# Dilated attention with every engine's queue in written order, and its small work handed out between dense products

## The chip, the cores and the metric

The kernel runs on one core of a Trainium2 chip. The metric is the device time of one execution in microseconds. A core has five engines with queues of their own, each worked off in order: TensorE (PE; its weight loads, PEld, overlap the matmuls), VectorE (DVE), ScalarE (ACT), GpSimd (POOL) and SyncE (SP). The last issues most DMAs here; ScalarE issues some too, and then does so from the same queue as its arithmetic. Engines wait for one another by semaphores. What stands behind a waiting instruction in a queue waits with it.

## The reference, cut to what matters

One encoder block with 1024 tokens of width 1024: a norm, one wide input projection, three mixers side by side (dilated window attention A, grouped-query attention B, cross-attention M), a gate for each, three merged projections, an output projection and a norm. The change is in mixer A:

```python
A_GROUPS = ((128, 1), (512, 4), (2048, 16))     # window, dilation
for gi, (window, dil) in enumerate(A_GROUPS):
    hs = slice(gi * A_HEADS, (gi + 1) * A_HEADS)
    o_g, lse_g = dilated_window_attention(aq[:, :, hs], ak[:, :, hs], av[:, :, hs], window, dil)
    ...
wts = jax.nn.softmax(jnp.stack(lses, axis=0), axis=0)
oa = jnp.einsum('gbsh,gbshd->bshd', wts, jnp.stack(outs, axis=0))
```

There are 8 heads of 64 channels in each group. Queries and keys are rotated by position (rope). In a group a query attends to the tokens at multiples of the dilation inside its window; the three groups' outputs are weighed by a softmax over their log-denominators.

## The kernel before

**Dense products in three passes.** Every float32 weight tile is split into a rounded high part and the rest (`split`, L104: a copy on ScalarE, a subtraction on VectorE), and so are the tokens. A unit (`add_unit`) is 128 output channels: two halves of 512 tokens, each 8 blocks of the width times three matmuls, so 24 matmuls (L143, L145, L147) into one of two PSUM banks `d`. Then the half is evacuated, and its bank is free again.

**The dilated stage** works through 12 items: four pairs of heads (`p_`), each in the three groups (`g` = 0, 1, 2). An item has eight tiles of 128 queries. For each tile there are: `scores` (four tiles at a time, TensorE, into four PSUM banks), `soft` (on VectorE the mask and the maximum; on ScalarE the exponential with its sum, for two heads), `trans` (TensorE turns the probabilities, ScalarE copies them out as `app`), and `pv` (values' products for four tiles, TensorE; ScalarE copies `og`). `stats` turns the row sums and maxima once for an item (L1359). The outputs of `trans`, `pv` and `stats` share two PSUM tiles. The transposes run two tiles behind the softmax, so the last two tiles, the second `pv` and the statistics of an item fall into the next one.

**What is woven.** `weave` (L174) sets TensorE's order by hand: it walks through the pieces of an item (`plan`, L1396), each with a cost, and through the matmuls of one dense unit, and takes the next matmul whenever the attention's share of its cost is ahead. The dense unit of item n makes the rotated queries of item n + 2 (`q_rope`: four products of 32 rows on VectorE, L1194, one of 128 rows, L1195, an addition on GpSimd, L1196); four gate units follow at the end. Keys come ready from HBM as two tiles (`kraw`, `kswp`), which GpSimd adds (`k_add`, L1223). Values come in blocks (`avs`, `avp`). After each third group, `combine` fetches the statistics, makes the weights (`weights`, L1471, a chain of short VectorE steps with one exponential on ScalarE), sends them through HBM (`wgd`, `wgt`) and weighs three outputs (`weigh`, L1491).

**What sets the order of the other engines.** The first two units run under a manual schedule, that is, in the order in which the code issues. All after it, to the end of the stage, is ordered on VectorE, ScalarE, GpSimd and SyncE by a scheduler that goes by priorities and estimated readiness; `issue_after` ties combining to the latest softmax step. The weights of a unit are loaded and split whole (1024 columns at once) when `prepare` reaches them, one unit ahead. Buffers `wr` for raw weights are two.

**The value stage**, earlier, from 456 us, makes the values with a scheme of seven block products. It starts with a write of reciprocals (`rld`, L829) from SyncE's queue, then eight weight loads `vA` (L857). `sum_at` (L894) issues its sums of weight blocks on GpSimd.

Of the kernel before, what the change touches and what calls it, by code (L numbers as in the profile page):

```python
# [16 lines left out]
NT = 8  # L17
# [33 lines left out]
def block(ctx: ExitStack, tc: tile.TileContext, x, xT, memT, cst, msk, bcst, tabA, gpost,  # L51
# [121 lines left out]

    def weave(count, att=None, att_cost=0.0, lead=1.0, prio=ATT_PRIO):  # L174
        dg = run_items(count)
        dc = cost_items(count)
        d = a = 0.0
        live_d, live_a = True, att is not None
        while live_d or live_a:
            if live_d and (not live_a or a / att_cost >= min(1.0, d / dc * lead)):  # L180
                try:
                    d += next(dg)
                except StopIteration:
                    live_d = False
                    d = 1e18
            else:
                try:
                    with tc.high_priority(offset=prio):
                        a += next(att)
                except StopIteration:  # L190
                    live_a = False
# [466 lines left out]
    with tc.tile_pool(name="ba", bufs=1, reuse_waits="tile") as ba:  # L658
# [170 lines left out]
        nc.sync.dma_start(rld.rearrange("h (a b) -> (h a) b", b=64), rl)  # L829
# [139 lines left out]

    BK = {}  # L970
# [58 lines left out]
    for n, (i, e, k) in enumerate(steps_v):  # L1029
# [76 lines left out]
    for n in range(6):  # L1106
        for i, (an, bn) in enumerate(PRODUCTS):
# [9 lines left out]
            if i == 0:  # L1117
                if n:
                    k_block(n, "S2")
                k_block(n, "A22")  # L1120
                if n < 5:
                    k_load(n + 1, 0)
            elif i == 1:
                k_block(n, "S4")
                if n < 5:
                    k_load(n + 1, 1)
            elif i == 2:
                k_block(n, "S1")
            elif n == 5:
                if i == 3:  # L1130
                    early[len(queue)] = lambda: [wp.tile([P, 1024], F32, name="wr", bufs=WR)]
                    prepare(len(queue))
                    nc.sync.dma_start(ready[len(queue)][0], wu[0])
                elif i == 6:
                    raw = ready.pop(len(queue))[0]
                    w = wslot(0), wslot(1)
                    split(*w, raw)
                    ready[len(queue)] = tuple(z.rearrange("p (k f) -> p k f", k=8) for z in w)
# [28 lines left out]
    with tc.tile_pool(name="aa", bufs=1, reuse_waits="tile") as aa:  # L1167
# [19 lines left out]
        def q_rope(o, half, p, g):  # L1187
# [4 lines left out]
            for a in range(4):  # L1192
                i, j = slice(32 * a, 32 * a + 32), slice(32 * (a ^ 1), 32 * (a ^ 1) + 32)
                V.scalar_tensor_tensor(t2[i], p[j], -0.125, tab[1][j, t], op0=OP.mult, op1=OP.mult)  # L1194
            fp["last"] = V.scalar_tensor_tensor(t1, p, -0.125, tab[0][:, t], op0=OP.mult, op1=OP.mult)  # L1195
            G.tensor_tensor(half_of(o, half, g), classes(t1, g), classes(t2, g), op=OP.add)  # L1196

        def add_a(p_, g):
# [7 lines left out]
            add_unit(wu[(p_ * 3 + g) * 2], evac)  # L1206
# [18 lines left out]
        def item(p_, g):  # L1225
# [130 lines left out]
            def stats():  # L1356
# [24 lines left out]
            size = [window(g, T)[1] - window(g, T)[0] for T in range(NT)]  # L1381
# [4 lines left out]
                scores=[(lambda b=b: scores(b), 350 + sum(size[4 * b:4 * b + 4]) * 4 / 2.4) for b in range(2)],  # L1386
                soft=[(lambda T=T: soft(T), 300.0) for T in range(NT)],
                trans=[(lambda T=T: trans(T), 109.0 * {128: 2, 192: 3, 256: 4}[size[T]]) for T in range(NT)],
                pv=[(lambda b=b: pv(b), 250.0 + sum(213.0 * len(blocks_of(T)) for T in range(4 * b, 4 * b + 4))) for b in range(2)],
                stats=(stats, 109.0))  # L1390

        def joined(*pieces):
            pieces = [x for x in pieces if x]
            return (lambda: [fn() for fn, _ in pieces]), sum(c for _, c in pieces)

        def plan(it, pre, nxt):  # L1396
# [3 lines left out]
            def combining(T):  # L1400
                while todo and T == STEP_T[-len(todo)]:
                    with tc.issue_after(fp["last"].ins):
                        todo.pop(0)()

            def tokens(T):
                if T >= 2:
                    for nm, k in late[:2]:
                        with tc.issue_after(fp["last"].ins):
                            split_block(nm, k)
# [109 lines left out]
        def first_blocks():  # L1519
            load_pair(0, 0)  # L1520
            load_pair(0, 1)
            own_blocks(0)

# [17 lines left out]
        seq = [(p_, g) for p_ in range(4) for g in range(3)]  # L1541
        add_a(*seq[0])
# [3 lines left out]
        k_fetch(*seq[0])  # L1546

        def first_keys():
            yield 300.0
# [4 lines left out]
            yield 300.0  # L1554

        weave(2, first_keys(), 1000.0)
        manual.__exit__(None, None, None)
        items = [item(*x) for x in seq] + [None]
        for n in range(len(seq)):
            if n + 2 < len(seq):  # L1560
                add_a(*seq[n + 2])
            elif n + 2 == len(seq):
                for j in GATES_A:
                    add_gate(*j)
                early[len(queue)] = first_blocks
# [13 lines left out]
            weave(len(GATES_A) - 1 if last else 1, run(pieces), sum(c for _, c in pieces), 1.0)  # L1579

# [335 lines left out]
G_AT = 4  # L1916
# [115 lines left out]
```

## Time and profile before

| what | value |
|---|---|
| median of 3 runs | 1476.32 us (1474.78 to 1477.55) |
| profiled execution, its own time | 1477.48 us |
| its span, first to last instruction | 1475.7 us |
| mean granted TensorE clock | 0.991 |
| TensorE busy | 1419.1 us, 96% of the span |
| VectorE, ScalarE, GpSimd busy | 998.7, 651.6, 523.1 us |
| dilated stage | about 706 to 1039 us |
| TensorE idle from 717 to 727 us | 9.8 us, one wait |
| TensorE idle from 741 to 1040 us | 19.5 us, 24 waits |

Times are counted from the first instruction. A busy share of TensorE includes matmuls at a lowered clock, so the granted clock (1.00 is full speed) belongs beside it. A group's row gives its line in the kernel, the engine, the operation, the output and inputs, the count, the busy time, the mean of one in ns, and the idle time just before it with what ended it. Line numbers are those of the kernel before; in the changed kernel the same code stands 6 lines lower in the value stage and some 15 to 55 lower in the dilated stage.

### The profile page before, as it was taken

The numbers are of one execution on the slowest core, as the hardware profiler recorded it, in microseconds if no ns is written. First come the engines' busy times: TensorE is split into PE (matmuls) and PEld (weight loads), VectorE is DVE, ScalarE is ACT, GpSimd is POOL, SyncE is SP. The second block draws the span as 40 slices with busy tenths as digits, with TensorE's granted clock in tenths as the row PEclk, the third lists the DMA queues.
The fourth block names the chain that finished last, engine by engine and source line by source line (L and its number), as shares of the span: only waits on it lengthen the run. The fifth ranks groups of instructions, "written<-read, shape, count | busy, mean of one in ns | idle before, by whom it ended". The sixth has DMA issues, their size and how long they took to land.

```text
span 1475.7 us, 21171 instructions
## 1 busy us (share of the span) xinstructions
PE 1419.1 (96%) x7556; PEld 1133.2 (77%) x7556; DVE 998.7 (68%) x1737; ACT 651.6 (44%) x1407; POOL 523.1 (35%) x402
## 2 busy tenths in 40 slices
PE   7999999999999899999799998999999999999998
PEld 7899986666666788888577767778887888888887
DVE  7755468777752974888565676675688788559643
ACT  6544365665653443321056564665433444213221
POOL 1425405676763402332143343430234331035322
PEclk9999999999999999999899999999999999999999
DMA  6332022223113688344533343453433543857122
GB/s 239 102 108 72 30 80 82 69 94 97 52 39 137 198 262 272 125 170 172 181 91 112 97 138 111 124 150 108 143 124 118 181 175 113 291 209 266 55 98 100
DMA packets 112985, 198.67 MB, mean 135 GB/s; under 512 B 23984, under 2 KB 53744, under 8 KB 112880
## 3 DMA queue, kind: packets, MB, share of 16 engines
q1 hardware_dynamic: 86816, 166.78, 34.5%
q10 hardware_dynamic: 26064, 30.55, 5.9%
q8 instruction: 59, 0.97, 0.3%
q14 instruction: 46, 0.38, 0.1%
HBM read 142.40 MB, written 54.89 MB: 134 GB/s over the span
## 4 chain that ended last, share of the span: by engine, by line
PE 68%; DVE 12%; ACT 7%; DMA 5%; issue 4%; POOL 3%; SPq 1%; ACTq 0%; DVEq 0%; POOLq 0%
PE s L125 16%; PE sc L125 9%; PE d L147 6%; PE d L145 6%; PE d L143 5%; PE sc L1878 5%; PE s L1040 4%; PE ov L755 3%; ACT pra L1303 3%; DVE t2a L1194 2%; PE s L739 2%; PE tr L721 2%; PE s L740 2%; PE d L536 2%; DMA wr<-in_wu 1%
## 5 line engine op out<-in xcount | busy, mean ns | idle before, releaser
L143 PE MATMUL d<-hh,wh 128*128 128x512 f32 x480 | 196.6, 410 | 11.5 <-DVE t1a L1195 9.8
L147 PE MATMUL d<-hh,wl 128*128 128x512 f32 x480 | 196.3, 409 | 0.0
L145 PE MATMUL d<-hl,wh 128*128 128x512 f32 x480 | 194.4, 405 | 0.0
L746 POOL TENSOR_TENSOR bl<-bl,bp 128x512 f32<-128x512 f32 x96 | 131.5, 1369 | 53.6 <-ACT bp L742 48.1
L105 ACT ACTIVATE wh<-wr 128x1024 fp32r<-128x1024 f32 (+1 forms) x75 | 67.3, 898 | 177.3 <-PE sc L125 76.0
L125 PE MATMUL sc<-hh,wh 128*128 128x512 f32 x384 | 118.4, 389 | 0.0
L143 PEld LDWEIGHTS d<-hh,wh 128*128 128x128 f32 x480 | 91.9, 191 | 33.0 <-issue 15.2
L145 PEld LDWEIGHTS d<-hl,wh 128*128 128x128 f32 x480 | 92.2, 192 | 21.6 <-issue 6.3
L147 PEld LDWEIGHTS d<-hh,wl 128*128 128x128 f32 x480 | 91.6, 191 | 22.1 <-issue 5.0
L1194 DVE SCALAR_TENSOR_TENSOR t2a<-d,tab 32x512 f32<-32x512 f32 x96 | 66.0, 687 | 56.6 <-PE d L147 54.9
L106 DVE TENSOR_TENSOR wl<-wr,wh 128x1024 fp32r<-128x1024 f32 x47 | 70.6, 1503 | 44.9 <-ACT wh L105 44.4
L1303 ACT ACTIVATE pra<-pra,sts 128x192 f32<-128x192 f32 (+2 forms) x192 | 84.2, 439 | 34.7 <-DVE sts L1302 34.6
L722 DVE TENSOR_REDUCE bn<-tr 128x1 f32<-128x512 f32 x128 | 86.1, 686 | 17.5 <-PE tr L721 16.1
L742 ACT ACTIVATE bp<-s 128x512 f32<-128x512 f32 x128 | 75.9, 595 | 46.8 <-PE s L740 45.7
L106 DVE TENSOR_TENSOR ch<-sf,ch 128x512 fp32r<-128x512 f32 x68 | 59.0, 869 | 44.4 <-ACT ch L105 44.3
L1196 POOL TENSOR_TENSOR aq<-t1a,t2a 128x512 f32<-128x512 f32 x24 | 43.8, 1825 | 123.7 <-DVE t1a L1195 103.7
L125 PEld LDWEIGHTS sc<-hh,wh 128*128 128x128 f32 x384 | 72.1, 188 | 15.1
L105 ACT ACTIVATE ch<-sf 128x512 fp32r<-128x512 f32 x68 | 41.6, 628 | 93.8 <-PE s L125 46.3
L1605 POOL TENSOR_TENSOR sf<-wr 128x512 f32<-128x512 f32 x22 | 30.6, 1409 | 144.2 <-DMA wr<-in_wu 61.4
L1809 POOL TENSOR_TENSOR acc<-acc,th 128x1024 f32<-128x1024 f32 x15 | 40.9, 2728 | 108.8 <-DVE th L1808 106.1
L125 PE MATMUL s<-hh,ch 128*128 128x512 f32 x224 | 74.1, 392 | 1.7 <-ACT ch L105 1.7
L125 PE MATMUL sc<-hl,wh 128*128 128x512 f32 x192 | 74.7, 389 | 0.0
(389 smaller groups left out, 3731.3 us busy)
## 6 DMA issues: line engine op xcount, KB each, us to landing
wr<-in_wu SPq DMA_DIRECT2D x64, 512.0 KB
kd<-kr ACTq DMA_DIRECT2D x48, 256.0 KB
th<-thd SPq DMA_DIRECT2D x24, 512.0 KB
thd<-rs ACTq DMA_DIRECT2D x44, 256.0 KB
g2d<-fth SPq DMA_DIRECT2D x24, 256.0 KB
kraw<-kd SPq DMA_DIRECT2D x12, 512.0 KB
kswp<-kd SPq DMA_DIRECT2D x48, 128.0 KB
wgt<-wgd SPq DMA_DIRECT2D x24, 256.0 KB
```

Of the source, the lines that this page charges most:

```text
L105: A.activation(dst_h, src, AF.Copy)
L106: V.tensor_tensor(dst_l, src, dst_h.bitcast(F32), op=OP.subtract)
L125: PE.matmul(out_ps, a, b, start=i == 0, stop=i == n - 1)
L143: PE.matmul(dst, wh[:, k, :], hh[k][:, t], start=k == 0, stop=False)
L145: PE.matmul(dst, wh[:, k, :], hl[k][:, t], start=False, stop=False)
L147: PE.matmul(dst, wl[:, k, :], hh[k][:, t], start=False, stop=k == 7)
L722: fp["last"] = V.tensor_reduce(st[i]["n"][:, j, c:c + 1], s, axis=AX.X, op=OP.min)
L742: A.activation(pp, s, AF.Exp, scale=-1.0)
L746: G.tensor_tensor(lsum[i % 2], lsum[i % 2], pp, op=OP.add)
L1194: V.scalar_tensor_tensor(t2[i], p[j], -0.125, tab[1][j, t], op0=OP.mult, op1=OP.mult)
L1303: A.activation(src, src, AF.Exp, scale=-1.0, bias=bias, accum_out=sts[:, h, 1, T:T + 1])
L1878: PE.matmul(parts[h], *terms[h][j], start=j == 0, stop=j == 23)
```

## The change

1. From the first two units to the end of the dilated stage, the manual schedule stays on for VectorE, ScalarE, GpSimd and SyncE: their queues hold the order in which the code issues. The `issue_after` ties and the empty piece before the statistics go.
2. A list `pend` takes small pieces: the five VectorE steps of each rotation, the two steps of each gate evacuation, and the next unit's weight split in two halves of 512 columns. `weave` issues the next of them after every third dense matmul.
3. The weights of the stage's 16 units have a list of their own (`AU`): each is fetched two units ahead, the first two already during the last key products; its split is handed out in the second half of the unit before.
4. The costs in `plan` no longer follow TensorE's time: a softmax step counts 1000, a joined piece (values' products and next scores) 300, a transpose 100. So the dense matmuls are spread over softmax steps.
5. In the value stage, the write `rld` goes out from ScalarE's queue, and the sums S3 and S4 are issued one step later.

```diff
+    pend = []
...
     def weave(count, att=None, att_cost=0.0, lead=1.0, prio=ATT_PRIO):
...
                     d += next(dg)
+                    steps += 1
+                    if pend and steps % 3 == 0:
+                        pend.pop(0)()
...
-        nc.sync.dma_start(rld.rearrange("h (a b) -> (h a) b", b=64), rl)
+        nc.scalar.dma_start(rld.rearrange("h (a b) -> (h a) b", b=64), rl)
...
+    def a_fetch(n):
+        AR[n] = wp.tile([P, 1024], F32, name="wr", bufs=WR)
+        nc.sync.dma_start(AR[n], wu[AU[n]])
+
+    def a_split(n, x):
+        if x == 0:
+            AW[n] = wslot(0), wslot(1)
+        split(*[z[:, half[x]] for z in AW[n]], AR[n][:, half[x]])
...
-        for nm, s0 in (("S1", 2), ("S3", 7), ("S4", 11)):
+        for nm, s0 in (("S1", 2), ("S3", 8), ("S4", 12)):
...
+            pend.extend([lambda a=a: cross(a) for a in range(4)] + [straight])
+
+        def add_au(evac):
+
+            n = next(counter)
+
+            def gen(_):
+                if n + 2 < len(AU):
+                    a_fetch(n + 2)
+                else:
+                    load_pair(0, n + 2 - len(AU))
+                for half in range(2):
+                    p = psd()
+                    if half and n + 1 < len(AU):
+                        pend.extend(lambda x=x: a_split(n + 1, x) for x in range(2))
+                    elif half:
+                        pend.append(lambda: own_blocks(0))
+                    w = [z.rearrange("p (k f) -> p k f", k=8) for z in AW[n]]
+                    yield from dense(w, half, p)
+                    evac(half, p)
+            queue.append((lambda: None, gen, UNIT))
...
-                soft=[(lambda T=T: soft(T), 300.0) for T in range(NT)],
-                trans=[(lambda T=T: trans(T), 109.0 * {128: 2, 192: 3, 256: 4}[size[T]]) for T in range(NT)],
+                soft=[(lambda T=T: soft(T), SOFT) for T in range(NT)],
+                trans=[(lambda T=T: trans(T), 100.0) for T in range(NT)],
...
-                    out += [(lambda: None, 300.0), pre["stats"]]
+                    out.append(pre["stats"])
...
         weave(2, first_keys(), 1000.0)
-        manual.__exit__(None, None, None)
...
+        while pend:
+            pend.pop(0)()
+        manual.__exit__(None, None, None)
...
+SOFT, JOINED = 1000.0, 300.0
```

**SyncE, where the dilated stage begins.** `in_wu` is the array of weights, `kd` holds the finished keys, `in_msk` the mask. Before:

```order
L1170 DMA mask<-in_msk 128x768
L1213 DMA kraw<-kd 128x1024
L1216 DMA kswp<-kd 32x1024 x4
L114 DMA wr<-in_wu 128x1024 x4
L1213 DMA kraw<-kd 128x1024
L1216 DMA kswp<-kd 32x1024 x4
```

Now, with the key stage's weight loads above the mask:

```order
L974 DMA wr<-in_wu 128x1024 x10
L982 DMA wr<-in_wu 128x1024 x3
L1185 DMA mask<-in_msk 128x768
L1266 DMA kraw<-kd 128x1024
L1269 DMA kswp<-kd 32x1024 x4
L1266 DMA kraw<-kd 128x1024
L1269 DMA kswp<-kd 32x1024 x4
L982 DMA wr<-in_wu 128x1024 x2
```

Three weight loads of this stage now stand ahead of the mask and of the first key tiles; before, all behind them.

**TensorE, around the statistics of an item** (`pra` are probabilities, `sts` the statistics). Before:

```order
L1329 MATMUL tr<-cs,pra 128x128 x4
L143 MATMUL d<-hh_87,wh 128x512
L145 MATMUL d<-hl_95,wh 128x512
L147 MATMUL d<-hh_87,wl 128x512
L1320 MATMUL tr<-cs,pra 128x128 x3
L143 MATMUL d<-hh_88,wh 128x512
L1359 MATMUL tr<-cs,sts 32x128
L145 MATMUL d<-hl_96,wh 128x512
```

Now:

```order
L1382 MATMUL tr<-cs,pra 128x128 x4
L143 MATMUL d<-hh_88,wh 128x512
L145 MATMUL d<-hl_96,wh 128x512
L147 MATMUL d<-hh_88,wl 128x512
L143 MATMUL d<-hh_89,wh 128x512
L145 MATMUL d<-hl_97,wh 128x512
L147 MATMUL d<-hh_89,wl 128x512
L1373 MATMUL tr<-cs,pra 128x128 x3
L1412 MATMUL tr<-cs,sts 32x128
```

Six dense matmuls stand between two tiles' transposes where there were three, and none before the statistics where there was one. The 12 to 14 that stood ahead of each values' product are now one or two.

**ScalarE at the same place** (two `pra` are one tile's exponentials, `app` the copy of turned probabilities, `sr` of the statistics). Before:

```order
L1354 ACTIVATE og<-tr 128x512
L1303 ACTIVATE pra,sts<-pra,sts 128x192 x6
L1332 ACTIVATE app<-tr 128x512
L1303 ACTIVATE pra,sts<-pra,sts 128x192
L1362 ACTIVATE sr<-tr 32x128
L1332 ACTIVATE app<-tr 128x384
```

Now:

```order
L1407 ACTIVATE og<-tr 128x512
L1356 ACTIVATE pra,sts<-pra,sts 128x192 x2
L1385 ACTIVATE app<-tr 128x512
L1356 ACTIVATE pra,sts<-pra,sts 128x192 x2
L1385 ACTIVATE app<-tr 128x384
L1415 ACTIVATE sr<-tr 32x128
```

The first copy stood behind three tiles' exponentials and now stands behind one tile's.

More of the change, by code (lines that the diff above doesn't have):

```diff
@@ L177, in weave @@
         d = a = 0.0
+        steps = 0
         live_d, live_a = True, att is not None
@@ L1129, in block @@
             elif n == 5:
[L1130 to L1138, printed above, removed]
+                for x_ in range(2 if i == 6 else 0):
+                    a_split(0, x_)
             elif i == 3:
@@ L1204, in evac, with add_ag, first, second @@
                 q_rope(d["q"], half, p, g)
-            add_unit(wu[(p_ * 3 + g) * 2], evac)
+            add_au(evac)
+        def add_ag(i, p_):
+            def evac(h, p):
+                th = aa.tile([P, 512], F32, name="fth", bufs=2)
+                def first():
+                    V.tensor_tensor(th, p, rb[:, half[h]], op=OP.mult)
+                    A.activation(p, th, AF.Tanh, scale=0.5)
+                def second():
+                    V.scalar_tensor_tensor(th, p, 1.0, th, op0=OP.add, op1=OP.mult)
+                    nc.sync.dma_start(g2d[i, p_, :, half[h]], th)
+                pend.extend([first, second])
+            add_au(evac)
         KK = {}
@@ L1401, in combining @@
                 while todo and T == STEP_T[-len(todo)]:
-                    with tc.issue_after(fp["last"].ins):
-                        todo.pop(0)()
+                    todo.pop(0)()
             def tokens(T):
@@ L1407, in tokens @@
                     for nm, k in late[:2]:
[L1408 to L1409 removed]
+                        split_block(nm, k)
                     del late[:2]
@@ L1563, in block @@
                 for j in GATES_A:
-                    add_gate(*j)
-                early[len(queue)] = first_blocks
+                    add_ag(*j)
             last = n + 1 == len(seq)
```

34 lines of the change are left out of this document (18 added, 16 removed).

## The prediction

> **What bounds the kernel now.** I read the page first, then the stretches of the dilated stage, then who TensorE waits for there.
>
> ```profile
> span 1475.7 us, 21171 instructions
> PE 1419.1 (96%) x7556; PEld 1133.2 (77%) x7556; DVE 998.7 (68%) x1737; ACT 651.6 (44%) x1407; POOL 523.1 (35%) x402
> ```
>
> TensorE sets the time: all that can be won without removing matmuls is the 56.6 us in which it is idle, and what a low clock costs after idling. The dilated stage runs from 706 to 1039 us. Per stretch (length, busy time of PE, PEld, DVE, ACT, POOL with instruction counts, then the granted clock, DMA share, GB/s):
>
> ```profile
> 717.00:727.00 10.00, 0.18 (x2) 0.03 (x1) 6.01 (x8) 2.11 (x2) 0.00 (x0) 0.71 0.52 176
> 727.00:742.00 15.00, 15.00 (x58) 11.98 (x58) 8.43 (x13) 1.07 (x1) 9.90 (x7) 0.86 0.25 76
> 742.00:780.00 38.00, 35.22 (x263) 28.15 (x264) 26.14 (x83) 20.81 (x71) 13.45 (x8) 0.96 0.33 98
> 780.00:857.00 77.00, 70.91 (x546) 55.85 (x546) 47.83 (x143) 44.48 (x146) 26.28 (x15) 0.98 0.41 114
> 857.00:928.00 71.00, 64.83 (x501) 51.00 (x497) 48.42 (x142) 40.24 (x133) 26.50 (x14) 0.98 0.43 121
> ```
>
> No helper is full: VectorE is busy 48 of 71 us where TensorE loses 6. So these are waits for order and latency. TensorE's waits between 741 and 1040 us (total, times, longest), and the one at the start:
>
> ```profile
> PE tr L1359 <- ACT app L1332: 12.3, 10, 2.8
> PE tr L1320 <- ACT app L1332: 3.1, 4, 1.3
> PE tr L1329 <- ACT app L1332: 2.5, 8, 0.5
> PE tr L1320 <- ACT pra L1303: 1.6, 2, 1.0
> PE d L143 <- DVE t1a L1195: 9.8, 1, 9.8
> ```
>
> **The start of the stage.** The 9.8 us have a cause in SyncE's queue:
>
> ```profile
> 709.41 0.33 SPq L1213 DMA_DIRECT2D kraw<-kd  x1
> 712.01 12.37 SPq L114 DMA_DIRECT2D wr<-in_wu  x4
> 719.74 1.06 ACT L105 ACTIVATE wh<-wr 128x1024 fp32r<-128x1024 f32 x1 [17.61 <-DMA wr<-in_wu]
> 720.83 1.23 DVE L106 TENSOR_TENSOR wl<-wr,wh 128x1024 fp32r<-128x1024 f32 x1 [10.30 <-ACT wh L105]
> ```
>
> The weights of the second unit stand behind the key tiles, which wait for the stage before; VectorE's split of them stands ahead of the first rotation, and that rotation holds the PSUM bank. After the wait the matmuls step by 0.43 us before they return to 0.23:
>
> ```profile
> 727.56 0.63 PE L145 MATMUL d<-hl,wh 128*128 128x512 f32 x1
> 727.99 0.63 PE L147 MATMUL d<-hh,wl 128*128 128x512 f32 x1
> ```
>
> From the clock 0.86 over 15.00 us that costs 15.00 x 0.14 = 2.1 us. The change fetches the first two units' weights during the key products, and puts the second split behind the first rotation: five steps of 0.69 us (rows below) and two half splits are 4.9 us beside the next 24 dense products of 0.23, 5.5 us. They fit. **Term 1: -9.8 - 2.1 = -11.9 us.** If the cover fails (the first scores then wait for the keys, which GpSimd adds only after those same transfers), up to all of it comes back.
>
> **The waits inside the stage.** Most are the statistics' transpose (L1359), which needs a PSUM tile that ScalarE's copy app frees. One such place:
>
> ```profile
> 904.52 0.46 ACT L1303 ACTIVATE pra<-pra,sts 128x192 f32<-128x192 f32 x1 [2.85 <-DVE sts L1302]
> 907.16 0.57 ACT L1332 ACTIVATE app<-tr 128x512 f32<-128x512 f32 x1
> 907.79 0.28 PE L1359 MATMUL tr<-cs,sts 128*32 128x128 f32 x1 [2.45 <-ACT app L1332]
> ```
>
> Six exponentials, three tiles' worth, stand in ScalarE's queue ahead of a copy whose input had been ready for long; the scheduler put them there. In the written order one tile's two exponentials stand there, and TensorE has five to six dense products between softmax steps where it had two or three. Recoverable: the four rows' 19.5 us; the clock, (1 - 0.96) x 35.22 + 0.02 x 70.91 + 0.02 x 64.83 = 4.1 us; and some 0.16 us for each of the 24 waits, since a matmul shows 0.39 us while the next may start 0.23 after it: 3.8 us. **Term 2: -27.4 us, before what the new order loses.**
>
> The Trainium skill ("TensorE: Matmul & The Clock Gate", "What's actually happening") lets the clock halve after an idle window of about 3.4 us. By that rule the waits of at most 2.8 us here would cost no clock, and the sum would lose the 4.1 us, giving an estimate of 1447; the clock rows at 742 to 928 us do not agree with it, so they are used.
>
> **What the new order loses.** Half a unit is the beat: 24 dense products, four softmax steps, one joined piece (values' products and scores). TensorE's price, from these rows:
>
> ```profile
> 770.80 0.49 PE L1320 MATMUL tr<-cs,pra 128*128 128x128 f32 x3
> 771.04 0.47 PE L143 MATMUL d<-hh,wh 128*128 128x512 f32 x1
> 771.36 0.39 PE L145 MATMUL d<-hl,wh 128*128 128x512 f32 x1
> 771.59 0.40 PE L147 MATMUL d<-hh,wl 128*128 128x512 f32 x1
> 914.61 1.75 PE L1346 MATMUL tr<-app,avs 128*64 128x128 f32 x28
> 918.25 0.50 PE L147 MATMUL d<-hh,wl 128*128 128x512 f32 x1
> ```
>
> Dense: 24 x 0.23 = 5.5. A step's transposes: 0.24 and 0.09 more before the next dense product, four times 1.3. Joined: 918.25 - 914.61 = 3.6. In all 10.4 us. VectorE's, by the rows of its groups (count | busy, mean ns | idle before), with one single instruction from the order of time among them:
>
> ```profile
> L1194 DVE SCALAR_TENSOR_TENSOR t2a<-d,tab 32x512 f32<-32x512 f32 x83 | 57.0, 687 | 50.0 <-PE d L147 48.5
> L1302 DVE CUSTOM_DVE_ANT_0 pra<-s,mask 128x192 f32<-128x192 f32 x80 | 24.4, 353 | 1.6 <-PE s L1290 0.8 <-PE tr L1320 0.2 <-ACT pra L1303 0.2
> L106 DVE TENSOR_TENSOR wgt<-wgt 128x512 fp32r<-128x512 f32 x3 | 2.0, 687 | 0.0
> L1494 DVE TENSOR_TENSOR og<-og,wgt 128x1024 f32<-128x1024 f32 x9 | 20.6, 2293 | 5.6 <-DMA wgt<-wgd 5.5
> 916.44 1.95 DVE L1494 TENSOR_TENSOR og<-og,wgt 128x1024 f32<-128x1024 f32 x1
> L1483 DVE TENSOR_TENSOR cds<-cds,cdn 128x16 f32<-128x16 f32 x3 | 4.0, 1335 | 0.1
> ```
>
> Five rotation steps 3.4, eight maxima 8 x 0.353 = 2.8, in every second half two half splits 1.4: at most 7.6 us of 10.4, a reserve of 2.8. So an ordinary half costs nothing. The exception is combining, three times: the weights (their largest step is 1.3 us; with the short ones and a round trip over ScalarE I take 3.5), two weighings 4.6, one 2.3, now in one in-order queue. Uncovered that is 3 x 10.4 = 31 us; fully covered 0. Beyond the reserve stand 0.7 + 1.8 + 0 = 2.5 us a time; the first weighing may also wait for its weights, whose path over HBM takes 3.4 us before it even starts to load:
>
> ```profile
> 903.74 1.27 SPq L1487 DMA_DIRECT2D wgd<-ceg  x2
> 907.12 0.49 SPq L1464 DMA_DIRECT2D wgt<-wgd  x1
> ```
>
> TensorE runs about two steps behind the maxima, so part of it never shows. I take 2 us a time, 6, and 2 for 24 halves' crumbs. **Term 3: +8 us (0 to 27.4).** Moved DMAs count too: value loads now stand behind the statistics' writes and the weight loads; that is a rival.
>
> The Trainium skill ("SBUF — State Buffer", "SBUF: two separate sides") says that VectorE with two SBUF inputs and GpSimd exclude each other for a whole instruction. The og rows agree (1.95 us for the single one, during which GpSimd ran nothing, against a mean of 2.29); it could lengthen weighings and splits, and lies inside term 3's bounds.
>
> **The value stage** (456 to 600 us). VectorE is late for TensorE by the sum of its waits:
>
> ```profile
> PE s L1040 <- DVE sl L106: 4.3, 4, 2.0
> PE s L1040 <- DVE wh L106: 0.9, 1, 0.9
> 486.00:496.00 10.00, 6.96 (x22) 5.27 (x23) 10.00 (x8) 1.87 (x3) 10.00 (x7) 0.83 0.25 82
> 464.36 0.33 SPq L827 DMA_DIRECT2D rl<-lbd  x1
> 467.30 3.77 SPq L857 DMA_DIRECT2D vA<-in_wv  x8
> ```
>
> Without the rld write in SyncE's queue the eight loads start after 464.7 instead of 467.30, 2.6 us earlier, and all that hangs on them. On ScalarE's queue the write waits for the reciprocal; behind it stands the split of vA, whose load has only just been issued by then, so it delays nothing. The clock, 0.17 x 6.96 = 1.2 us, recovers in part. **Term 4: -3 us** (0 if VectorE's own work beside GpSimd sets the lateness, -6.4 if all goes). The later S3 and S4 leave GpSimd's order there as it was: 0, or no more than the 0.9 us row either way.
>
> **Sum.** The profiled execution took 1477.5 us (span 1475.7, the rest around it), 1.2 above the runs' median of 1476.3. 1477.5 - 11.9 - 27.4 + 8 - 3 = 1443.2; I take **1443**.
>
> **Rivals.** *Nothing is lost*: reserve and lag cover combining too (term 3 at 2) and the value stage gives 5: 1477.5 - 39.3 + 2 - 5 = 1435. For it, VectorE's 2.8 us of reserve; against it, the in-order wait for the weights. *The inner waits stay*: the transposes merely change what they wait for, because maxima and rotations now share one fixed order (term 3 at 27): 1477.5 - 11.9 - 3 = 1463. For it, the same two-step lag and two PSUM tiles; against it, VectorE's fill. *The start's wait moves* to the first scores, waiting for the keys' addition on GpSimd; at half of term 1: 1449. For it, the key transfers still start only after 709. *Slower*: the value blocks, loaded only after the values' products before, arrive late. From there TensorE has the scores, 3.6 - 1.75 = 1.9, and 5.5 + 1.3 to the next use, 8.7 us. Five issues at 0.63 (the wgd row has two in 1.27) take 3.2, so a landing over 5.5 us makes a wait in each of 11 items, and from 3.1 us of wait on (34.3 / 11, a landing of 8.6) the kernel is slower: at 4 us, 1443 + 44 = 1487. Against it, no wait for a DMA stands among the rows before. *The change does not do what it says* (the dense products still bunch) is excluded by the order of instructions.
>
> **Chances.** Forecast 0.50, nothing lost 0.15, inner waits stay 0.16, start moves 0.12, slower 0.04, no change by a mixture of these 0.03. A measurement of this kernel tells about 0.2% from none, 3 us. Faster 0.93, same 0.03, slower 0.04. Range 1435 to 1463: from the fully covered case to the one in which the inner waits stay.
>
> **What would show it.** Term 1: dense products without a break from 706 to 728 us and no matmul at 0.43. Term 2: L1359's transpose (now L1412) no longer among the waits, granted clock 1.00 throughout. Term 3: what waits remain sit in the second item of each three, behind the weighings. Term 4: the vA loads at 465 and waits of some 2.5 us there. A wait of TensorE for avs or avp, or for the addition ak, would prove me wrong, as would VectorE filled over 95% for whole items.

## The result: faster by 1.7%, 8 us less than forecast

The changed kernel takes 1451.05 us (median of 4 runs, 1448.28 to 1454.76), the kernel before on the same chip 1476.76: a ratio of 0.9829, 95% interval 0.9805 to 0.9854. Forecast were 1443 us and a range of 1435 to 1463. The profiled execution took 1451.03 us. Two executions of the variants below (2136 us of the write from GpSimd's queue, 1749 us of en bloc) ran at a far lower granted clock and are left out. From the page of the change:

```profile
span 1449.2 us, 21150 instructions
...
PE 1411.5 (97%) x7556; PEld 1134.1 (78%) x7556; DVE 1003.7 (69%) x1753; ACT 656.4 (45%) x1423; POOL 526.8 (36%) x402
```

TensorE's busy time fell by 7.6 us with the same number of matmuls, while the mean granted clock rose from 0.991 to 0.997. The rest of the gain is idle time. The stretches of the dilated stage now (columns as in the prediction), and who TensorE waits for from 741 to 1040 us:

```profile
703.00:735.00 32.00, 32.00 (x159) 26.04 (x159) 25.86 (x50) 6.40 (x20) 13.78 (x8) 1.00 0.66 207
...
726.00:794.00 68.00, 68.00 (x523) 55.83 (x522) 46.05 (x153) 44.99 (x151) 30.34 (x16) 1.00 0.44 121
794.00:857.00 63.00, 57.73 (x462) 46.95 (x460) 47.33 (x129) 36.62 (x119) 25.69 (x13) 0.97 0.50 130
857.00:925.00 68.00, 64.80 (x505) 52.66 (x505) 51.91 (x149) 42.28 (x142) 27.52 (x14) 1.00 0.46 120
```
```profile
PE tr L1399 <- DMA avs<-vdr: 6.7, 3, 3.7
PE tr L1399 <- ACT app L1385: 1.3, 1, 1.3
PE tr L1399 <- DMA avp<-vdr: 0.8, 2, 0.5
PE tr L1412 <- ACT app L1385: 0.6, 1, 0.6
PE tr L1399 <- ACT wh L105: 0.3, 1, 0.3
PE tr L1373 <- ACT app L1385: 0.3, 1, 0.3
```

The first 90 us of the stage have no gap at all. TensorE's waits for ScalarE from 741 to 1040 us, 19.5 us before, are down to 2.5. In their place stand five waits for value blocks, 7.5 us: the sign that the prediction said would prove it wrong. Between landmarks of the two traces:

| stretch | before, us | after, us | difference | forecast |
|---|---|---|---|---|
| to the first dense product of the dilated stage | 706.1 | 703.4 | -2.7 | -3 |
| from there to the first scores | 35.8 | 22.3 | -13.5 | -11.9 |
| first scores to the stage's last value product | 296.5 | 282.6 | -13.9 | -19.4 |
| from there to the last stage's first product | 213.2 | 216.8 | +3.6 | 0 |
| from there to the end | 224.1 | 224.1 | 0 | 0 |

In the new order, six dense products (1.4 us) that stood ahead of the first scores stand behind them. So the start gained 13.5 - 1.4 = 12.1 us and the inside 13.9 + 1.4 = 15.3. Two things were not foreseen: the inside gives 4 us less, and a stretch that the change doesn't touch is 3.6 us longer.

### The profile page after: what moved, and what is told of

It is laid out like the page before. It is cut to its first block, busy times and chain, and to the rows that moved or that the text cites. A ratio compares the mean times of both kernels' runs of the same rounds, so it can differ in the third digit from the quotient of the medians.

```text
span 1449.2 us, 21150 instructions
## 1 busy us (share of the span) xinstructions
PE 1411.5 (97%) x7556; PEld 1134.1 (78%) x7556; DVE 1003.7 (69%) x1753; ACT 656.4 (45%) x1423; POOL 526.8 (36%) x402
## 4 chain that ended last, share of the span: by engine, by line
PE 73%; DVE 9%; DMA 5%; ACT 5%; issue 4%; POOL 3%; SPq 1%; ACTq 0%; POOLq 0%; DVEq 0%
PE s L125 16%; PE sc L125 9%; PE d L145 6%; PE d L143 6%; PE d L147 5%; PE s L1059 5%; PE sc L1926 5%; PE ov L761 3%; PE s L745 2%; PE tr L727 2%; PE s L1343 2%; PE s L746 2%; PE d L542 2%; PE d L1059 2%; PE tr L1399 1%
## 5 line engine op out<-in xcount | busy, mean ns | idle before, releaser
L147 PE MATMUL d<-hh,wl 128*128 128x512 f32 x480 | 193.2, 402 | 0.0
L145 PE MATMUL d<-hl,wh 128*128 128x512 f32 x480 | 191.4, 399 | 0.0
L105 ACT ACTIVATE wh<-wr 128x512 fp32r<-128x512 f32 (+1 forms) x91 | 68.8, 773 | 141.6 <-PE sc L125 78.4
L106 DVE TENSOR_TENSOR wl<-wr,wh 128x512 fp32r<-128x512 f32 (+1 forms) x63 | 83.4, 1342 | 60.1 <-ACT wh L105 59.9
L145 PEld LDWEIGHTS d<-hl,wh 128*128 128x128 f32 x480 | 90.5, 189 | 22.4 <-issue 6.5
L1209 DVE SCALAR_TENSOR_TENSOR t2a<-d,tab 32x512 f32<-32x512 f32 x96 | 66.0, 687 | 24.4 <-PE d L147 22.3
L1857 POOL TENSOR_TENSOR acc<-acc,th 128x1024 f32<-128x1024 f32 x15 | 40.9, 2727 | 112.6 <-DVE th L1856 109.8
```

The costliest lines, as they stand in the source:

```text
L105: A.activation(dst_h, src, AF.Copy)
L106: V.tensor_tensor(dst_l, src, dst_h.bitcast(F32), op=OP.subtract)
L145: PE.matmul(dst, wh[:, k, :], hl[k][:, t], start=False, stop=False)
L147: PE.matmul(dst, wl[:, k, :], hh[k][:, t], start=False, stop=k == 7)
```

## Experiments

All times are medians of four runs (three for the write from GpSimd's queue and for en bloc, five for the last kernel of the table); the ratio is against the kernel before on the same chip. The kernels ran on several chips, on which the kernel before took 1475.1 to 1476.9 us, so times of different rows compare to some 2 us only. "Inside" is first scores to last value product in the profiled execution; a dash means that no trace is read.

| kernel | us | ratio (interval) | inside, us |
|---|---|---|---|
| the change | 1451.05 | 0.9829 (0.9805 to 0.9854) | 282.6 |
| keys later | 1450.07 | 0.9835 (0.9807 to 0.9863) | 283.5 |
| combined pair's write later | 1443.83 | 0.9794 (0.9767 to 0.9822) | 274.1 |
| both | 1449.53 | 0.9828 (0.9805 to 0.9850) | 280.0 |
| that write from GpSimd's queue | 1445.44 | 0.9790 (0.9769 to 0.9812) | - |
| old costs | 1448.71 | 0.9830 (0.9805 to 0.9856) | 278.6 |
| old costs, write later | 1449.45 | 0.9822 (0.9804 to 0.9841) | 278.6 |
| en bloc, write later | 1449.55 | 0.9822 (0.9799 to 0.9845) | 281.8 |
| weights late | 1453.99 | 0.9855 (0.9836 to 0.9874) | 278.2 |
| reciprocals' write back | 1450.31 | 0.9836 (0.9813 to 0.9858) | 279.8 |
| write later, unused tile | 1442.65 | 0.9780 (0.9762 to 0.9797) | 276.6 |
| write later, five banks, keys added apart | 1442.04 | 0.9785 (0.9758 to 0.9812) | 275.3 |
| write later, five banks | **1440.72** | 0.9762 (0.9742 to 0.9781) | 274.5 |

### Why the value blocks are late

At the longest wait, SyncE's queue and TensorE read as follows in the changed kernel (start, duration, engine, line; a row of several issues includes the waits between them):

```profile
834.95 0.35 SPq L1550 DMA_DIRECT2D od<-og  x1
835.39 0.38 SPq L982 DMA_DIRECT2D wr<-in_wu  x1
835.82 0.78 SPq L1266 DMA_DIRECT2D kraw<-kd  x1
836.65 1.88 SPq L1269 DMA_DIRECT2D kswp<-kd  x4
838.62 8.41 SPq L1429 DMA_DIRECT2D std<-sr  x8
847.14 1.23 SPq L1293 DMA_DIRECT2D avs<-vdr  x2
```
```profile
852.37 1.91 PE L1399 MATMUL tr<-app,avs 128*64 128x128 f32 x16 [3.71 <-DMA avs<-vdr]
```

The write `od` of a combined head pair must wait until GpSimd has added the third output; everything behind it in the queue waits too. SyncE's waits in the stage (total, times, longest) put a figure on it:

```profile
SPq L1537 <- DVE ceg L1535: 28.3, 3, 9.4
SPq L1550 <- POOL og L1548: 24.5, 3, 9.7
...
SPq L1425 <- DMA kraw<-kd: 6.3, 2, 3.6
```

Two rows are longer in total: L1537, the write of the weights, and the weight loads (L982, 33.9 us for VectorE's maxima). They are as long in the run with the write moved below (28.3 and 40.9), in which hardly a wait for values is left; so they are not the cause. Of the 7.5 us that TensorE waits for values, 5.5 (3.7 and 1.8) stand behind the write `od`; the other 2.0 stand in items without it.

Three candidates: the stop at this write, the key loads ahead of the statistics' writes and the values, and (the prediction's third term) VectorE's weighings. First the key loads were moved:

```diff
-                if it and it["ahead"] and T in (1, 5):
+                if it and it["ahead"] and T in (4, 7):
...
-                (k_fetch if T == 1 else k_add)(*key)
+                (k_fetch if T == 4 else k_add)(*key)
```

> The changed kernel with the key loads of the item after next issued at the fifth step (behind the value loads) and their addition at the eighth, instead of the second and the sixth. Theory V, what the new order loses is lost because the value blocks' loads stand in SyncE's queue behind five key loads, the weight rows and the statistics' writes: the loads of avs and avp go out 2 to 6 us earlier, the waits for them in the dilated stage (7.5 us in the trace of the changed kernel) fall under 2 us, and the time is 1445 us (1443 to 1448). Rival W, the weighings on VectorE lose it (the third term of the prediction): the waits are only renamed, 1451 within 3 us. Rival K: the keys' addition now meets the combining's additions on GpSimd and scores wait for ak: 1455 or more.

Measured: 1450.07 us, no change. Yet theory V's first half came true: no wait for avs or avp is left. Waits for ScalarE's copies have taken their place:

```profile
PE tr L1412 <- ACT app L1385: 6.4, 4, 2.5
PE tr L1373 <- ACT app L1385: 1.4, 1, 1.4
```

Why, the order of time shows ahead of the longest one, VectorE and GpSimd side by side:

```profile
809.05 1.82 DVE L1530 TENSOR_TENSOR cdn<-ceg,cpt 128x48 f32<-128x48 f32 x1 [0.42 <-ACT ceg L1528]
810.90 1.93 DVE L1532 TENSOR_TENSOR cds<-cdn 128x16 f32<-128x16 f32 x1
812.87 0.17 DVE L1533 TENSOR_TENSOR cds<-cds,cdn 128x16 f32<-128x16 f32 x1
```
```profile
808.84 3.96 POOL L1276 TENSOR_TENSOR ak<-kraw,kswp 128x512 f32<-128x512 f32 x2 [3.72 <-DMA kswp<-kd]
```

The moved key addition runs beside the chain of weights. Two steps of 48 and 16 numbers a partition take 1.82 and 1.93 us, each as long as one of GpSimd's two instructions (1.98); the next, with GpSimd done, takes 0.17. The Trainium skill ("SBUF — State Buffer", "SBUF: two separate sides") says that a VectorE operation with two SBUF inputs and a GpSimd operation that reads SBUF lock each other out for a whole instruction; the trace agrees, with 1.82 and 1.93 us beside 1.98. In VectorE's written order the next maxima stand behind the chain, so the statistics' transpose is late again.

Next the write alone, behind the values of the next item (the last pair's, with no item behind it, stays):

```diff
-                if g == 2:
-                    nc.sync.dma_start(od[0, p_], ogs[0])
+                if g == 2 and p_ == 3:
+                    write()
+            def write():
+                nc.sync.dma_start(od[0, p_], ogs[0])
-            return [fetch, weights] + [lambda g=g: weigh(g) for g in range(3)]
+            return [fetch, weights] + [lambda g=g: weigh(g) for g in range(3)] + [write]
...
-        STEP_T = (4, 7, 3, 3, 7)
+        STEP_T = (4, 7, 3, 3, 7, 4)
```

> The changed kernel with the write of a combined head pair moved from the eighth step of one item to the fifth of the next, behind the value loads, so that SyncE's queue no longer stops for GpSimd's sum (9.7 us in the trace of the changed kernel) ahead of the next item's loads. Theory V: the waits for avs in the third item of each three (3.7 and 1.8 us) go, those of the second item (1.5 us) stay: 1445.5 us (1444 to 1448). Rival W, the weighings on VectorE: 1451 within 3 us.

Measured: 1443.83 us (1442.21 to 1445.07); its slowest run is faster than the fastest of the change. The same place now, the values' loads ahead of the write and 4.7 us earlier, and the stretch that had lost most:

```profile
836.80 5.55 SPq L1429 DMA_DIRECT2D std<-sr  x8
842.47 1.23 SPq L1293 DMA_DIRECT2D avs<-vdr  x2
843.79 0.56 SPq L1553 DMA_DIRECT2D od<-og  x1
```
```profile
794.00:857.00 63.00, 62.21 (x493) 50.60 (x492) 48.81 (x143) 41.19 (x136) 27.13 (x15) 1.00 0.51 137
```

VectorE's work is the same as before the edit, so the weighings did not lose these 7 us (the ratio falls from 0.9829 to 0.9794, and to 0.9780 in a repeat of the same program, below). The order of value loads and `od` changed too, so the queue's stop was tested by itself: the write stays in its place but goes out from GpSimd's queue.

```diff
-                    nc.sync.dma_start(od[0, p_], ogs[0])
+                    nc.gpsimd.dma_start(od[0, p_], ogs[0])
```

> The changed kernel with the combined head pair's write where it was, but issued from GpSimd's queue, right behind the addition it waits for, instead of SyncE's. Theory V, it is SyncE's stop at this write that makes the value blocks late: the time falls as with the write moved behind the next values, 1444 us (1442 to 1446). Rival, the place of the write's traffic among the loads is what counts, not the queue's stop: 1450 within 2 us. Rival, the issue costs GpSimd so much that the key additions are late: over 1451.

Measured: 1445.44 us (1444.9 to 1445.54), ratio 0.979 as with the write moved. This rests on the times alone. Theory V holds: it is SyncE's stop, not the place of the write's traffic.

Both moves in the queue together:

> Both moves in SyncE's queue together: keys loaded behind the values, the combined head pair written behind the values of the next item. Theory V: no wait for avs or avp of 1 us or more is left, 1443 us (1441 to 1446), the two gains overlap in the third items and do not add. Rival W: 1451 within 3 us. Rival K (GpSimd late with ak): 1453 or more.

Measured: 1449.53 us. Theory V was wrong here, for the reason that the keys' run showed, and rival W's number has another cause. Again no wait for avs, again the statistics' transpose, and again two steps of the chain beside GpSimd:

```profile
806.94 1.45 DVE L1524 TENSOR_TENSOR cmn<-cpt 128x16 f32<-128x16 f32 x1
808.43 1.90 DVE L1525 TENSOR_TENSOR cmn<-cmn,cpt 128x16 f32<-128x16 f32 x1
```

To separate the key loads from their addition, the last run loads the keys late but adds them in the third step of the next item (on top of the fastest kernel below):

```diff
+                if it and T == 2 and n_ and n_ - 1 + 2 < len(seq):
+                    out.append((lambda: k_add(*seq[n_ + 1]), 0.0))
+                if it and it["ahead"] and T == 4:
+                    out.append((lambda: k_fetch(*it["ahead"]), 0.0))
```

> The fastest kernel so far (1440.7 us: combined head pair written behind the next values, five accumulator banks), with the keys loaded behind the values as in the run with the keys later, but added on GpSimd in the third step of the next item, apart from the chain of weights in the eighth step. Theory, the 6 us that the later keys cost (1443.8 to 1449.5 with the write moved) come from GpSimd's addition beside that chain: two of its small VectorE steps take 1.8 and 1.9 us instead of 0.2 in the trace with the keys later. With the addition apart these steps are short, no transpose of statistics waits 1 us or more, and the time is 1440.5 us (1439 to 1442.5). Rival, the later key loads themselves cost it: 1445 or more.

Measured: 1442.04 us (1441.25 to 1444.32). In the stage these steps are back at 0.17 to 0.21 us, no wait at L1412 reaches 1 us, and the loss of 6 us is gone: it came from the addition beside the chain, not from the loads. The later loads bring nothing either (1440.72 without them; ratios 0.9785 and 0.9762, intervals overlapping).

### What each part of the change brings

The planner's costs of before, all else as changed:

```diff
-                soft=[(lambda T=T: soft(T), SOFT) for T in range(NT)],
+                soft=[(lambda T=T: soft(T), 300.0) for T in range(NT)],
...
-            return (lambda: [fn() for fn, _ in pieces]), JOINED
+            return (lambda: [fn() for fn, _ in pieces]), sum(c for _, c in pieces)
```

> The changed kernel with the planner's costs of before (a softmax step 300, scores, transposes and value blocks by their own lengths, the filler of 300 ahead of the statistics); queues in written order and handed-out rotations and splits stay. Theory A, the gain inside the dilated stage needs both: with the old costs two or three dense products again stand between two groups of transposes and twelve to fourteen ahead of a value block, so transposes wait for their softmax steps: the waits of the first 14 or so us come back, about 1465 us (1458 to 1472). Rival B, the written order alone brings it: 1451 within 3 us.

Measured: 1448.71 us. Theory A was wrong: the gain comes without the spreading. This run keeps the written order, the handing out and the early fetch. All of TensorE's waits from 741 to 1040 us:

```profile
PE d L143 <- DVE t1a L1212: 7.8, 3, 2.6
PE tr L1373 <- ACT app L1385: 0.2, 1, 0.2
```

Three times, once per combined pair, a dense product waits for a bank that VectorE's rotation frees, because the weighings delay it: two of them, 3.9 us together, run on VectorE just ahead of that rotation. The values that TensorE waited for in the change come in time here. One of the three places, with the old costs:

```profile
885.52 0.50 PE L143 MATMUL d<-hh,wh 128*128 128x512 f32 x1 [2.58 <-DVE t1a L1212]
885.86 0.40 PE L145 MATMUL d<-hl,wh 128*128 128x512 f32 x1
...
909.68 1.23 SPq L1293 DMA_DIRECT2D avs<-vdr  x2
916.11 1.09 PE L1399 MATMUL tr<-app,avs 128*64 128x128 f32 x16
```

The same item in the change:

```profile
914.60 1.23 SPq L1293 DMA_DIRECT2D avs<-vdr  x2
919.82 1.09 PE L1399 MATMUL tr<-app,avs 128*64 128x128 f32 x16 [1.81 <-DMA avs<-vdr]
```

From the issue to the product it took 5.2 us in the change, and TensorE waited for it; with the old costs TensorE comes 6.4 us after the issue and need not wait. Without the 2.6 us that it had lost before, it would have come 3.8 us after, some 1.4 too early (an estimate from these rows). So one wait covered the other, and with the stop at `od` the spreading only swapped them; this is argued from the rows. Then the spreading should count once the stop is gone:

> The write of the combined pair behind the next value loads and the planner's costs of before, together. Theory, the spreading gives nothing and the moved write gives its 7.2 us: 1441.5 us (1439 to 1444). Rival, the old costs' waits of the dense products for the rotations (7.8 us in the trace with the old costs alone) are no part of SyncE's queue and stay, while the gain of the moved write is partly hidden behind them: 1446 to 1449.

Measured: 1449.45 us; the theory (two gains that add) was wrong, the rival right. The three waits of 2.6 us stay, and moving the write brings nothing (inside 278.6 us in both). Without the stop the spreading is worth 1449.45 - 1443.83 = 5.6 us, or 6.8 against the repeat of the same program on this run's chip (1442.65, below); with it, nothing.

The handing out, tested on the kernel with the write moved ("en bloc": all pieces at once):

```diff
-                    if pend and steps % 3 == 0:
+                    while pend:
                         pend.pop(0)()
```

> The kernel with the combined head pair's write behind the next value loads (1443.8 us), with the second part of the change undone: each rotation's five steps, each gate's two and each split's two halves are issued at once instead of one after every third dense product. Theory, the handing out carries part of the gain: five steps of 0.69 us put 3.4 us in front of the next maxima in 22 halves, of which the two steps of lag cover most: 1448 to 1452. Rival, the lag covers all: 1444 within 2 us. Rival, handing out is the heart of the change: the transposes wait again, 1460 or more.

Measured: 1449.55 us (1448.46 to 1451.75), within the theory's range: the handing out is worth 5.7 us by the times, 4.1 by the ratios. The transposes wait again, though nowhere near as before:

```profile
PE tr L1382 <- ACT app L1385: 6.7, 7, 1.8
PE tr L1373 <- ACT app L1385: 2.2, 2, 1.3
PE tr L1399 <- ACT app L1385: 0.9, 4, 0.2
```

### The start and the value stage

```diff
-                    a_fetch(0)
-                    a_fetch(1)
...
             k_fetch(*seq[0])
+            a_fetch(1)
...
             k_fetch(*seq[1])
+            a_fetch(2)
```

(The first unit's fetch goes to where it stood, two slots later.)

> The changed kernel with the early weight fetch of the dilated stage undone: the first query unit's weights are loaded two slots later in the last key group, the second unit's behind the first key loads, the third's behind the second key loads; written order and spreading stay. Theory, the first term of the prediction: the second unit's weights arrive late again, the stage's first products stand still about 10 us, and the time is 1463 us (1459 to 1465). Rival: the written order alone (rotations in short pieces, key additions behind them) makes the start, 1451 within 3 us.

Measured: 1453.99 us, 3 more than the change (intervals overlapping), and not 12. TensorE waits once at the start, for the weights' copy, and then steps by 0.43 us for 3 us:

```profile
718.99 0.50 PE L143 MATMUL d<-hh,wh 128*128 128x512 f32 x1 [3.55 <-ACT wh L105]
...
720.74 0.63 PE L145 MATMUL d<-hl,wh 128*128 128x512 f32 x1
721.17 0.63 PE L147 MATMUL d<-hh,wl 128*128 128x512 f32 x1
```
```profile
703.00:735.00 32.00, 28.45 (x126) 22.53 (x125) 22.14 (x32) 2.31 (x4) 11.80 (x7) 0.95 0.54 169
```

The first scores come 6.7 us later (732.4 instead of 725.7), 1.0 of it already at the stage's first product (704.4 instead of 703.4). So the early fetch is worth 5.7 us, about half of the start's 12.1. The rest comes with the written order. As before, one key load stands ahead of these weights; but the first rotation no longer stands behind their split. Its first step before, and its first four steps in this run, before the second unit's weights had come:

```profile
722.08 0.68 DVE L1194 SCALAR_TENSOR_TENSOR t2a<-d,tab 32x512 f32<-32x512 f32 x1
```
```profile
710.04 2.79 DVE L1210 SCALAR_TENSOR_TENSOR t2a<-d,tab 32x512 f32<-32x512 f32 x4 [1.18 <-PE d L147]
```

So TensorE waits 3.55 us for the weights, where before it waited 9.8, first for the weights and then for the rotation. Inside, this run is 4.4 us shorter than the change, 1.9 of it by fewer waits for avs and avp (5.6 us instead of 7.5); the rest is not explained, and two traces of one program differ by 2.5 (below).

```diff
-        nc.scalar.dma_start(rld.rearrange("h (a b) -> (h a) b", b=64), rl)
+        nc.sync.dma_start(rld.rearrange("h (a b) -> (h a) b", b=64), rl)
```

> The changed kernel with one line undone: the reciprocals' write goes back to SyncE's queue ahead of the value loads. Theory, the fourth term of the prediction: the vA loads go out about 2.6 us later, the value stage is 2.5 us longer, 1453.5 us. Rival: the shift of the two sums by one step already covers it, the value stage stays at 241.8 us from its first product to the first dense product of the dilated stage, 1451.

Measured: 1450.31 us, the rival's number, but the theory's trace. The loads `vA` go out at 467.13 us instead of 464.60. The dense products of the dilated stage up to 760 us, first of this kernel, then of the change (count, durations in ns, first and last start):

```profile
L143 PE MATMUL d<-hh,wh x57: 387/389/499, 706.5 to 757.0; 128*128 128x512 f32 x57
```
```profile
L143 PE MATMUL d<-hh,wh x59: 387/389/499, 703.4 to 759.4; 128*128 128x512 f32 x59
```

These products start 3.1 us later (1.8 to 3.1 against all the other runs, 703.4 to 704.7), and the inside of the dilated stage is 2.8 us shorter, with 4.7 us of waits for avs and avp instead of 7.5. That would fit value loads which come when SyncE's queue lets them, so that time won ahead is partly waited away. It is not shown: the change's own runs differ by 6.5 us, and two traces of one program by 2.5 inside.

### The unforeseen 2.2 us before the last stage

Between the weight products and the last stage's first product (sc) TensorE now waits 2.2 us, in the change and in each variant with six banks; the rows are those of the change:

```profile
PE s L125 <- ACT ch L105: 2.7, 3, 1.6
PE sc L125 <- ACT rs L1683: 2.2, 1, 2.2
```

Before, there was no row for sc, and the other stood at 1.7. In the built programs the accumulator banks turn in another order after the dilated stage: the last weight product lies in bank 4 before and in bank 3 after, and the last stage's first tile takes banks 2 and 3 in both. Two edits on the kernel with the write moved:

```diff
     phase_psum("ps_w", s1=6)
+    pss1()
```

> The kernel with the combined head pair's write behind the next value loads (1443.8 us), and one unused accumulator tile taken at the start of the weight products' stage, so that the last stage's first scores get another pair of banks. If the 2.2 us that the first of these products waits for the tanh of the last gates come from the banks' turn, the wait goes and the time is 1441.6 us; if it comes from an operand, the wait stays and so does 1443.8.

Measured: 1442.65 us, and the wait stays. The edit did not do what it should: the built program is the same, instruction for instruction and bank for bank, so it tells nothing about the cause. It is a repeat of the kernel with the write moved, on another chip, and shows how far a repeat lies off: 1442.65 against 1443.83 us, and 276.6 against 274.1 inside.

```diff
-    phase_psum("ps_w", s1=6)
+    phase_psum("ps_w", s1=5)
```

> The kernel with the combined head pair's write behind the next value loads (1443.8 us), with five accumulator banks instead of six in the stage of the weight products. The last product before the last stage then lies in a bank that the first scores do not take. Theory, the 2.2 us there are the wait for a bank that two late evacuations free: no wait in that place, 1441.6 us (1440.5 to 1443). Rival, five banks cost the stage's own products more than 2 us (new waits of products for evacuations): 1444 or more.

Measured: 1440.72 us (1439.57 to 1442.9), the fastest kernel here. With five banks the last weight product lies in bank 6, no row for sc is left, and the stretch is 213.8 us long (213.2 before the change, 215.6 with the write moved alone). Its page and what is left of TensorE's waits from 741 to 1040 us:

```profile
span 1438.1 us, 21169 instructions
...
PE 1409.4 (98%) x7556; PEld 1132.8 (79%) x7556; DVE 996.6 (69%) x1753; ACT 656.4 (46%) x1423; POOL 525.1 (37%) x402
```
```profile
PE tr L1399 <- ACT app L1385: 1.3, 1, 1.3
PE tr L1399 <- DMA avp<-vdr: 1.2, 2, 0.6
PE tr L1412 <- ACT app L1385: 0.5, 1, 0.5
```

## Why the prediction was right, and where it was wrong

**Direction and range: right.** TensorE's idling in the dilated stage was order and latency, not a full helper, and the change removed most of it. That the written order did it is left over by elimination: undoing one of the other parts at a time cost 7 us at the most, and no run takes the written order alone away. That 1451 lies inside the range is in part luck: the range was as wide as term 3's bounds, and term 3 came out large by another mechanism than the one it was reckoned from.

**Term 1** (-11.9): -12.1 in the trace, with dense products unbroken from 703 to 726 us. The size was right; its cause only half. Late weights alone do not make it: undoing the fetch brings 5.7 us back.

**Term 2** (-27.4): the statistics' transpose went from 12.3 us of waiting to 0.6, all of TensorE's waits for ScalarE to 2.5. The granted clock is 1.00 in every stretch shown but one (0.97 from 794 to 857 us), where 1.00 throughout was forecast. The working that tied it to five to six dense products per softmax step was not needed: the run with the old costs, which puts two or three there, has 0.2 us of such waits.

**Term 3** (+8) is the step that failed. It measured 27.4 - 15.3 = 12.1, taken as what is missing from term 2 in full, and it was put on the wrong engine. VectorE's reserve of 2.8 us did cover the weighings, thanks to the spreading; without it they cost three times 2.6. What was lost came from SyncE's queue. The prediction named the mechanism, late value blocks, as its slower rival, but priced it from the issue rows alone (3.2 us for five issues) as one wait in each of 11 items. The trace has five waits in four items, second and third ones of a combined pair. What delays most of them is rare: a write that waits for GpSimd, once per combined pair, behind which 5.5 of the 7.5 us stand; the third such write in the stage cost no wait. I had listed what was queued ahead of the value loads and not what each of those entries waits for. With the stop gone term 3 measures 4 to 6: in the three traces of that order the inside is 274.1, 274.5 and 276.6 us, which is 22.4, 22.0 and 19.9 less than before, and 1.4 more with the moved products.

**Term 4** (-3): -2.5 by the trace (waits on VectorE in the value stage 5.2 us before, 3.0 after), 1.8 to 3.1 by its undoing, and the loads `vA` start at 464.60 us as forecast; in the time it could not be seen.

**Left out**: the last stretch's +3.6. 2.2 of it is the bank's turn, shown by its removal; the rest, 1.4, lies within what that stretch differs by from run to run (214.9 to 216.8 in the variants with six banks).

The sum by the traces: -2.7 - 12.1 - 15.3 + 3.6 = -26.5, 1475.7 to 1449.2. Of the rivals, "nothing is lost" (1435) is not reached even by the fastest kernel (1440.72), which lies nearer the forecast of 1443; "inner waits stay" is refuted by the waits, "the start's wait moves" by the unbroken start. "Slower" had the right mechanism and, with one wait in each of 11 items, the wrong number of them.

## What to carry to other kernels

When queues go into written order, go through each one and note, for every entry, what it waits for; an entry that waits for a slow engine belongs behind the loads that the next products need, or into the queue of the engine it waits for. An improvement measured beside such a stop can read as nothing: the spreading was worth nothing with it and some 6 us without. And before a helper's work is moved in time, look at what the other engine on the same memory does there.

## What the runs showed of the hardware

- A VectorE step on 16 numbers a partition took 0.17 us alone and up to 1.93 us beside GpSimd's addition, and in the run with both moves the two cmn groups took 11.5 us where they take 2.5 in the change. The prediction had this as 17% of a long weighing (2.29 against 1.95); for a chain of short steps it is a factor of ten.
- Idling of 2.2 to 2.6 us lowers TensorE's clock sometimes. In the run with the old costs the wait of 2.61 us was followed by a matmul of 0.63 us, the one of 2.58 shown above by one of 0.40. The wait of 2.20 us before the last stage stands in all ten traces read of kernels with six banks. In four of them (keys later, both, old costs with and without the write moved) matmuls step by some 0.4 us soon after it, and from there to the end it takes 225.8 us; in the other six it takes 224.1 to 224.2. The same wait so costs 1.6 us or nothing. The Trainium skill ("TensorE: Matmul & The Clock Gate", "What's actually happening") has a free-running window of about 3.4 us, whose phase would explain that some waits count and others don't. No run here shows the window, and the waits that lowered the clock were shorter than it; there the measurement decides.
- An issue in SyncE's queue can wait for the landing of a load that it has nothing to do with: L1425's writes of statistics stood 6.3 us for kraw in the row of SyncE's waits above. This is the program's doing: as built, its transfers use eight semaphores in turn, and an issue waits until the transfer that used its semaphore before has landed. So a stop in the queue also passes on through the landings behind it; how much of the loss went that way, no run separates.
